# A transformer trunk on one core: the mixed stretch ordered by a planner in the kernel, plain products in a bank of the sevens

## The chip, the cores and the metric

The kernel runs on one core of a Trainium2 chip. The metric is the time of one execution on the device in microseconds (us), as the median of three runs. TensorE (PE) multiplies and loads its weights (PEld), VectorE (DVE), ScalarE (ACT) and GpSimd (POOL) do the elementwise work, and SyncE (SP) issues most of the transfers from the chip's memory.

## What is computed

Two layers of an encoder for 256 tokens of width 2048, in float32. Cut to what matters:

```python
for l in range(DEPTH):                      # 2
    h = rms_norm(x, ln1_g[l])
    o = two_attentions(h @ w_in[l])         # 8 + 8 heads of 128
    x = x + o @ w_out[l]
    h2 = rms_norm(x, ln2_g[l])
    u = depthwise_conv(h2 @ w_up[l], conv_w[l], conv_b[l])
    gate, up = u[..., :5632], u[..., 5632:]
    x = x + (silu(gate) * up) @ w_down[l]
```

The weights are most of the 412.80 MB that one execution reads.

## The kernel before

**Quanta and portions.** The weights come in quanta of 128 x 2048 numbers (1 MB), listed in `quanta` in the order in which TensorE uses them. A quantum is used in portions of 128 x 1024: two halves, or three *parts* for a seven. `steps` lists the portions. For each one TensorE needs a *high* part, the weight rounded to TensorE's fast 32-bit type, and a *low* part, the weight minus its high part. ScalarE makes the high part (tile `whi`, L114 or L807) and VectorE the low part (tile `wlo`, L115). For the second half of each plain and of the second quantum of each up, the low part comes another way (`by_transfer`): ScalarE writes the negated weight into `v_a` or `v_b` (L794), and GpSimd issues a DMA that adds the weight to it (L795), with the rounded sum as the low part. Activations are split in the same way, so a product of weights and activations takes three multiplications: high by high, low by high, high by low.

**The loop.** In step s, `low_w` prepares the low part by transfer of step s + 7 and `split_w` both parts of step s + 4 (five buffers each of `whi` and `wlo`). Three quanta are in SBUF at a time (`raw`); when the last portion of one is split, SyncE may load the next but two (L767), as soon as its tile is released.

**The feed-forward part.** A value of f, 0 to 43, stands for 128 columns of the gate and 128 of the other half. An *up* is two quanta: 32 matmuls of 512 and 32 of 256 columns into a tile `mm` of PSUM, the up's pair of banks. Then `glu` follows: ScalarE reads the pair into two tiles `prob` (L558, L559), VectorE adds them and scales them into `halo` (L560, L561), GpSimd copies the two halo edges (L563, L564), ScalarE and VectorE do the convolution (L569 to L573), then SiLU and gate, and the result is split into a *middle* tile. There are 26 middle tiles in five places (`MIDDLE`). For each pair of f, `sums_mid` makes four sums of the gated values (L589 to L592).

**Sevens and plains.** For the first 32 values of f, and in one half of the columns for 8 more, the product with `w_down` takes a form with seven products in place of eight, in chunks of eight f and for two halves m of the columns. One *seven* handles a pair of f in three parts of six matmuls, each 512 wide. VectorE makes the sums of its weights in place (L773 to L775, before part 1 is split). Four sevens add up in seven banks of PSUM: products 1 and 6 are the two banks of one tile `mm`, 5 and 7 take `S`, 3 takes `tr`, 4 takes `pv`. Then `add_seven` (L636 to L644) adds the banks to x: ScalarE copies product 1 (L637) into `tq`, VectorE reads the rest. The products with the fourth block of the weights are left to a *plain*, one quantum and 12 matmuls for each chunk and m, into a bank of its own in a tile `mm` (of which there are two, shared with the ups and sevens), and VectorE adds it to x (L673).

**The order.** In the list, nine ups come first. Then for each m the plain stands ahead of four pairs of a seven and an up:

```python
while f < PART + 1:
    quanta += up(f)
    f += 1
...
for m in range(2):
    quanta += plain(m)
    for i in range(PAIRS):
        quanta += seven(i, m) + up(f)
        f += 1
```

The last chunk (12 values of f) has one plain and four sevens, and its other products are `down` quanta. I call the time from the tenth up to the first `down` the *mixed stretch*; there is one in each layer. On each engine the instructions stand in an order that the scheduler of the language sets when the program is built, by its own estimate of durations and by the priorities in the code (`tc.high_priority`). The engines then run them in that order.

## Time and profile before

| what | value |
|---|---|
| median of three runs | 2200.76 us (2199.34 to 2203.48) |
| profiled execution | 2200.82 us |
| its span, first to last instruction | 2199.0 us |
| mean granted TensorE clock | 0.991 |
| PE busy | 2106.3 us, 96% |
| PEld busy | 1779.7 us, 81% |
| DVE busy | 1720.6 us, 78% |
| ACT busy | 1539.4 us, 70% |
| POOL busy | 221.8 us, 10% |

The profile is one execution, recorded instruction by instruction. A row of a group names a line, an engine, an operation, its output and inputs (the names of their tiles) and the shape, then how often it ran, how long together and on average. "A <- B: 24.6, 8, 3.5" in a view of waits says that A stood idle 24.6 us in all, in 8 places, 3.5 us at most, each time ended by B. PE's busy time counts overlapping matmuls as busy, so 96% does not mean that 4% is all that could be won. A view of windows gives the busy time of every engine in a stretch of the span.

### The profile page before, as it was taken

To read this page: it belongs to the slowest core of one execution; us is meant where nothing else is said; L and a number is where in the kernel's file an instruction comes from. 1 tells how busy PE (TensorE), PEld (TensorE's weight loads), DVE (VectorE), ACT (ScalarE), POOL (GpSimd) and SP (SyncE) were. 2 spreads that over 40 slices of the span, in tenths; PEclk is the share of its full clock that TensorE was granted. 3 is DMA by queue.
4 is the path that set the end of the run, shared out by engine and by line. 5 is a ranking of instruction groups with operands and counts; after the bars stand their busy time and mean duration, and the time that the engine had idled before them with its cause. 6 is when DMAs were issued, how large, how long until landed. Compare 5 with 4: busy or idle time off the path is not lost.

```text
span 2199.0 us, 29611 instructions
## 1 busy us (share of the span) xinstructions
PE 2106.3 (96%) x10720; PEld 1779.7 (81%) x10720; DVE 1720.6 (78%) x2522; ACT 1539.4 (70%) x2419; POOL 221.8 (10%) x343
## 2 busy tenths in 40 slices
PE   9999999999899998998999999999999999889999
PEld 7888888887778777777888888888877788777877
DVE  7786656778888888888857866667898889888886
ACT  7566558877777777777655665588777777777774
POOL 0011101110100001001000111011100001011000
PEclk9999999999999999999999999999999999999999
DMA  9555467776776677767655454577777777767774
GB/s 349 173 167 171 164 190 223 223 251 223 223 228 221 220 230 230 228 211 225 243 182 182 156 175 163 185 223 218 262 226 230 230 229 237 224 211 231 258 225 154
DMA packets 78563, 472.40 MB, mean 215 GB/s; under 512 B 9168, under 2 KB 11728, under 8 KB 29136
## 3 DMA queue, kind: packets, MB, share of 16 engines
q1 hardware_dynamic: 62432, 413.85, 52.1%
q0 software_dynamic: 15264, 55.58, 13.9%
q8 instruction: 84, 1.38, 0.2%
q10 hardware_dynamic: 720, 1.08, 0.1%
q14 instruction: 63, 0.52, 0.1%
HBM read 412.80 MB, written 2.10 MB: 189 GB/s over the span
## 4 chain that ended last, share of the span: by engine, by line
PE 48%; DMA 22%; DVE 19%; ACT 6%; issue 5%; ACTq 0%; SPq 0%; POOLq 0%; DVEq 0%
PE mm L100 42%; DVE wlo L115 9%; DMA raw<-in_w_up 9%; DMA raw<-in_w_seven 5%; DMA raw<-in_w_plain 4%; ACT whi L114 4%; DMA v_b<-raw 2%; DVE raw L773 2%; DMA v_a<-raw 2%; PE pv L100 2%; PE S L100 2%; DVE pT L573 1%; DVE raw L775 1%; PE tr L377 1%; DVE mid L115 1%
## 5 line engine op out<-in xcount | busy, mean ns | idle before, releaser
L115 DVE TENSOR_TENSOR wlo<-raw,whi 128x1024 fp32r<-128x1024 f32 (+1 forms) x739 | 893.1, 1221 | 336.0 <-ACT whi L114 307.9
L100 PE MATMUL mm<-xs,whi 128*128 128x512 f32 x2816 | 987.2, 393 | 8.4 <-ACT prob L559 8.1
L114 ACT ACTIVATE whi<-raw 128x1024 fp32r<-128x1024 f32 (+1 forms) x739 | 765.1, 1052 | 328.8 <-PE mm L100 182.2
L100 PEld LDWEIGHTS mm<-xs,whi 128*128 128x128 f32 x2816 | 530.5, 188 | 126.3 <-ACT prob L559 17.4
L100 PE MATMUL mm<-xs,wlo 128*128 128x256 f32 x2112 | 599.8, 284 | 2.7 <-DVE wlo L115 2.6
L100 PEld LDWEIGHTS mm<-xs,wlo 128*128 128x128 f32 x2112 | 401.8, 190 | 12.0 <-DVE wlo L115 10.0
L100 PE MATMUL mm<-whi,mid 128*128 128x512 f32 x1032 | 290.0, 404 | 48.6 <-DVE tq L638 30.0
L100 PE MATMUL mm<-whi,xs 128*128 128x512 f32 x1152 | 294.9, 393 | 1.3 <-ACT whi L114 1.2
L100 PEld LDWEIGHTS mm<-whi,mid 128*128 128x128 f32 x1032 | 195.8, 194 | 97.7 <-DVE tq L638 33.8
L100 PEld LDWEIGHTS mm<-whi,xs 128*128 128x128 f32 x1152 | 213.0, 188 | 43.7 <-ACT whi L114 2.2
L100 PE MATMUL mm<-wlo,xs 128*128 128x512 f32 x576 | 158.8, 393 | 0.0
L100 PE MATMUL mm<-wlo,mid 128*128 128x512 f32 x480 | 149.2, 399 | 3.8 <-DVE wlo L115 3.8
L571 ACT ACTIVATE pT<-halo,conv 128x256 f32<-128x256 f32 x352 | 149.4, 496 | 3.6 <-POOL halo L563 3.5
L573 DVE TENSOR_TENSOR pT<-pT 128x512 f32<-128x512 f32 x176 | 121.3, 689 | 30.2 <-ACT pT L571 25.9
L100 PEld LDWEIGHTS mm<-wlo,xs 128*128 128x128 f32 x576 | 107.2, 188 | 21.4
L807 ACT ACTIVATE whi<-raw 128x1024 fp32r<-128x1024 f32 x106 | 111.3, 1050 | 2.6 <-PE mm L100 2.0
L100 PEld LDWEIGHTS mm<-wlo,mid 128*128 128x128 f32 x480 | 91.4, 191 | 25.1 <-DVE wlo L115 6.2
L100 PE MATMUL mm<-xs,v_b 128*128 128x256 f32 x352 | 99.3, 282 | 0.0
L100 PE MATMUL mm<-xs,v_a 128*128 128x256 f32 x352 | 99.3, 282 | 0.0
L794 ACT ACTIVATE v_a<-raw 128x1024 fp32r<-128x1024 f32 x53 | 55.9, 1056 | 60.8 <-DMA raw<-in_w_up 42.6
L795 POOL DMA_DIRECT2D v_a<-raw x53 | 46.2, 871 | 508.0 <-ACT v_a L794 340.2
L795 POOL DMA_DIRECT2D v_b<-raw x53 | 46.1, 870 | 502.7 <-ACT v_b L794 343.0
(223 smaller groups left out, 2529.2 us busy)
## 6 DMA issues: line engine op xcount, KB each, us to landing
raw<-in_w_up SPq DMA_DIRECT2D x176, 1024.0 KB, 6.3
raw<-in_w_seven SPq DMA_DIRECT2D x72, 1024.0 KB, 5.7
raw<-in_w_in SPq DMA_DIRECT2D x71, 1024.0 KB, 4.9
raw<-in_w_out SPq DMA_DIRECT2D x32, 1024.0 KB, 4.9
v_a<-raw POOLq DMA_DIRECT2D x53, 512.0 KB, 4.8
v_b<-raw POOLq DMA_DIRECT2D x53, 512.0 KB, 4.9
raw<-in_w_plain SPq DMA_DIRECT2D x18, 1024.0 KB, 5.9
raw<-in_w_down SPq DMA_DIRECT2D x16, 1024.0 KB, 4.9
```

The source lines that it names most:

```text
L100: nc.tensor.matmul(ps, lhsT, rhs, start=start, stop=stop, skip_group_check=True)
L114: high = nc.scalar.activation(hi, src, AF.Copy)
L115: nc.vector.tensor_sub(lo, src, hi.bitcast(F32))
L377: nc.tensor.transpose(ps[:, kt, tt * P:(tt + 1) * P], p[:, tt, kt * P:(kt + 1) * P], ident)
L571: nc.scalar.activation(n[:, j, :], ux[:, j, o:o + T], AF.Copy, scale=w)
L573: nc.vector.tensor_add(y, y, n)
L773: nc.vector.tensor_sub(w[:, 1:3], w[:, 1:3], w[:, 2:4])
L775: nc.vector.tensor_sub(w[:, 0], w[:, 3], w[:, 0])
L794: nc.scalar.activation(lo, src, AF.Copy, scale=-1.0)
L795: nc.gpsimd.dma_start(out=lo, in_=src, accum_op=ALU.add)
L807: highs[s] = nc.scalar.activation(hl[s][0], raw[q][:, half * 1024:(half + 1) * 1024], AF.Copy)
```

## The change

A class `Plan` keeps a list of the instructions to come on each engine, with what they need, an estimated cost and a time at which they are due. It takes one at a time: of those that can begin within 0.1 us of the earliest on their engine, the one due first. Within the mixed stretch (from f = 1 of each layer to the first `down`) the order of PE, ACT, DVE and POOL is what it puts out (`tc.manual_schedule`); SP's stays the scheduler's. The other edits:

- The plain of a pair of chunk and m comes after its four sevens, and multiplies into the bank of product 1 (`cur["seven"][1]`), once ScalarE has copied that product (`copy_seven`, after part 0 of the last seven). Its own addition to x is gone. The nine additions of `add_seven` are each due at a time of their own.
- The halo edges are copied by ScalarE, in two instructions (`sides`).
- A quantum is loaded in two halves of 512 KB, into six tiles of half the size, and inside the mixed stretch a seventh in the place of `tabs`, a table of attention. `kT` holds a sixth high part. The sums of a seven's weights become four instructions of 512 columns in place of one of 1024 and two of 512, with results in `prob_a`, which GpSimd clears again for each layer.
- Three middle tiles fewer (23); three of a pair's four are given back early. Eight ups come first, not nine. `EARLY` is 6.

The numbers of instructions: TensorE's matmuls stay at 10632. VectorE's TensorTensor go from 2031 to 2085, ScalarE's ACTIVATE from 2317 to 2493, SyncE's transfers from 430 to 815, GpSimd's copies from 176 to 0.

The diff, cut to its core:

```diff
-MIDDLE = (("mid", MIDS), ("qT", 3), ("qtok", 3), ("kT", 2), ("kTb", 1))
+MIDDLE = (("mid", MIDS), ("qT", 3), ("qtok", 3))
-EARLY = 7
+EARLY = 6
...
+    def act(self, key, n, due, fn, deps=(), pointers=0, when=None):
+        self.op(key, "ACT", 0.12 + 0.00084 * n + 0.09 * pointers, due, fn, deps, when)
+
+    def dve(self, key, n, due, fn, deps=(), k=1, when=None):
+        self.op(key, "DVE", k * (0.075 + 0.00105 * n), due, fn, deps, when)
+
...
+    def run(self, stop):
+        while stop in self.ops:
+            best = {}
...
+            for eng, c in best.items():
+                first = min(c)[0] + 0.1
+                due, t, key = min((due, t, key) for t, due, key in c if t <= first)
+                if pick is None or t < pick[0]:
+                    pick = t, key
+            t, key = pick
+            eng, dur, _, fn, _, _ = self.ops.pop(key)
+            self.free[eng] = t + dur
+            self.now = self.done[key] = t + dur + self.LATE
+            fn()
...
-        nc.gpsimd.tensor_copy(ux[:, :, 1:r], ux[:, :, T:T + r - 1])
-        nc.gpsimd.tensor_copy(ux[:, :, T + r:T + 2 * r - 1], ux[:, :, r + 1:2 * r])
...
+        def scale():
+            nc.vector.tensor_mul(ux[:, :, r:r + T], own[0], st["r2"][:, None, :].to_broadcast([P, 2, T]))
+
+        def sides():
+            nc.scalar.activation(ux[:, :, 1:r], ux[:, :, T:T + r - 1], AF.Copy)
+            nc.scalar.activation(ux[:, :, T + r:T + 2 * r - 1], ux[:, :, r + 1:2 * r], AF.Copy)
...
+        plan.act(k("t"), 512, e + 2.5, lambda: read(0), [("pe", q, 1), k("gate", f - 1)])
+        plan.act(k("t2"), 512, e + 3.0, lambda: read(1), [k("t"), k("sum", f - 1)])
+        plan.dve(k("sum"), 512, e + 5.0, lambda: nc.vector.tensor_add(own[0], own[0], own[1]), [k("t"), k("t2")])
+        plan.dve(k("scale"), 512, e + 6.0, scale, [k("sum")] + [k(n + str(j), f - 2) for n in "yab" for j in range(2)])
+        plan.op(k("sides"), "ACT", 0.3, e + 7.0, sides, [k("scale")])
...
+                plan.act(k(n + str(j)), T, e + 7.5 + i % 3 + 0.5 * j, lambda n=n, j=j, o=o, i=i: tap(n, j, o, i),
+                         [k(dep), old], 2 if n == "y" else 1)
...
+        plan.dve(k("gate"), T, e + 14.0, gate, [k("silu")] + old)
+        plan.act(k("high"), T, e + 18.0, high, [k("gate")], when=lambda: sum(free.values()) > 0)
+            todo = (((1, gs[f][:, :, a], 1), (3, ss[p, 3], 0)),
+                    ((7, ss[p, 2], 0), (5, ss[p, 0], 1)),
+                    ((4, gs[f + 1][:, :, b], 0), (6, ss[p, 1], 1)))[part]
...
-                    drop(l, p)
+                    drop(l, p, (0, 2, 3))
                 if i == PAIRS - 1:
-                        add_seven(m, ps)
+                    add_seven(l, c, m, q, ps)
+            if part == 0 and i == PAIRS - 1:
+                copy_seven(l, c, m, q, ps)
...
+    def copy_seven(l, c, m, q, ps):
...
+            nc.scalar.activation(cur["t"], ps[1], AF.Copy)
+
+        plan.act(k("copy"), 512, ends.get(q, 0.0) - 2.2, copy, [("pe", q, 0), k("x2_", 1)])
...
+    def add_seven(l, c, m, q, ps):
...
+        last = [("pe", q + 1, 1)]
...
-        nc.vector.tensor_add(x11, x11, ps[1])
-        nc.scalar.activation(t, ps[1], AF.Copy)
-        nc.vector.tensor_add(t, t, ps[6])
-        nc.vector.tensor_add(x12, x12, t)
-        nc.vector.tensor_add(x12, x12, ps[3])
-        nc.vector.tensor_add(x_2, x_2, both(ps[5]))
-        nc.vector.tensor_add(t, t, ps[7])
-        nc.vector.tensor_add(x2_, x2_, both(t))
-        nc.vector.tensor_sub(x21, x21, ps[4])
+        add = nc.vector.tensor_add
+
+        plan.dve(k("x12b"), 512, e + 11.0, lambda: add(x12, x12, ps[3]), [("pe", q, 2)])
+        plan.dve(k("x_2"), 1024, e + 13.4, lambda: add(x_2, x_2, both(ps[5])), [("pe", q, 2), k("x12b")])
+        plan.dve(k("x11"), 512, e + 11.5, lambda: add(x11, x11, ps[1]), last)
+        plan.dve(k("t6"), 512, e + 12.0, lambda: add(cur["t"], cur["t"], ps[6]), last + [k("copy")])
+        plan.dve(k("x12"), 512, e + 13.6, lambda: add(x12, x12, cur["t"]), [k("t6"), k("x_2")])
+        plan.dve(k("t7"), 512, e + 14.0, lambda: add(cur["t"], cur["t"], ps[7]), [k("x12")])
+        plan.dve(k("x2_"), 1024, e + 22.0, lambda: add(x2_, x2_, both(cur["t"])), [k("t7"), k("x_2"), k("x21")])
+        plan.dve(k("x21"), 512, e + 15.0, lambda: nc.vector.tensor_sub(x21, x21, ps[4]), [("pe", q, 2)])
...
-            if half == 0:
-                cur["dn"] = psum.tile([P, TT, 512], F32, name="mm", bufs=2)
-            ps = cur["dn"][:, 0]
+            ps = cur["seven"][1]
...
-                       half == 0 and i == 0 and x_part == 0 and w is hv, half == 1 and i == 1 and w is lv)
-            if half == 1:
-                xv = x[:, 0, m * 1024:m * 1024 + 512]
-                nc.vector.tensor_add(xv, xv, ps)
...
-            while f < PART + 1:
...
+            while f < PART:
                 quanta += up(f)
                 f += 1
-            if nf == PART:
-                for m in range(2):
-                    quanta += plain(m)
-                    for i in range(PAIRS):
-                        quanta += seven(i, m) + up(f)
-                        f += 1
-            else:
-                quanta += plain()
+            for m in range(2 if nf == PART else 1):
                 for i in range(PAIRS):
-                    quanta += seven(i)
+                    quanta += seven(i, m)
+                    if i == PAIRS - 1:
+                        quanta += plain(m)
                     if f < NF:
                         quanta += up(f)
                         f += 1
...
-            raw[q] = wp.tile([P, 2048], F32, name="raw", bufs=3)
...
+    def load(parts=1, home="raw"):
+        if loaded[0] < len(halves):
+            q, h = k = halves[loaded[0]]
+            loaded[0] += 1
...
+                raw[k] = wp.tile([P, 1024], F32, name="raw", bufs=HALVES)
...
-        if part == 1:
-            nc.vector.tensor_sub(w[:, 1:3], w[:, 1:3], w[:, 2:4])
-            nc.vector.tensor_add(w[:, 3], w[:, 3], w[:, 1])
-            nc.vector.tensor_sub(w[:, 0], w[:, 3], w[:, 0])
-        return split(hv, lv, (w[:, 1::2], w[:, 1:3], w[:, 0::3])[part])
...
+    def free_raw(k):
+        del raw[k]
+        home = homes.pop(k)
+        if home == "raw" or plan.active:
+            load(1, home)
...
+    def sums_first(q):
+
+        zs[q] = act.tile([P, 3 * TT * T], F32, name="prob_a")[:, 0:1024]
+        z, u, w = pair(zs[q]), pair(raw[q, 0]), pair(raw[q, 1])
+        nc.vector.tensor_sub(z[:, 0], u[:, 0], w[:, 0])
+        nc.vector.tensor_sub(z[:, 1], w[:, 0], u[:, 1])
+
+    def sums_second(q):
...
+        nc.vector.tensor_add(u[:, 1], u[:, 1], z[:, 0])
+        nc.vector.tensor_sub(u[:, 0], u[:, 1], w[:, 1])
+        free_raw((q, 1))
...
+        plan.act(high, 1024, due - HI, lambda: high_w(s), need + prev + full, when=here)
+        plan.dve(low, 1024, due - LO, lambda: low_w_dve(s), [high] + order[-1:] + slot())
...
+        if kind == "seven" and part == 0:
+            plan.dve(("z", q), 512, due - Z1, lambda: sums_first(q), from_raw + [("raw", q, 1)] + zlast, 2, when=both)
+            zlast[:] = [("low_w", s + 1), ("z2", q)]
+            plan.dve(("z2", q), 512, due - Z2, lambda: sums_second(q), [("z", q), high, low], 2)
...
+        if kind == "plain":
+            l, c, m = a
+            return w + [("copy", l, 2 * c + m)] + list(needs_plain(l, c, part))
+        return w
...
+            region.enter_context(tc.manual_schedule(engines={
+                mybir.EngineType.PE, mybir.EngineType.Activation, mybir.EngineType.DVE, mybir.EngineType.Pool}))
+            start_plan(s)
...
+        if plan.active:
+            if ("pe", q, half) in plan.ops:
+                plan.run(("pe", q, half))
+        else:
+            low_w(s + EARLY)
+            split_w(s + SPLIT_AHEAD - 1)
+            split_w(s + SPLIT_AHEAD)
```

**In the program.** The rows below stand at one place on three engines: layer 0, the end of the first four sevens (m = 0 of the first chunk). Names end in the number of the tile.

TensorE before: the last two matmuls of an up (xs are its activations), then the plain, whose tile mm_4797 is its own.

```order
L100 MATMUL mm_4686<-xs15_3109,whi_4662 128x512
L100 MATMUL mm_4686<-xs15_3109,v_b_4578 128x256
L100 MATMUL mm_4797<-whi_4682,mid_3320 128x512
L100 MATMUL mm_4797<-whi_4682,mid_3553 128x512
L100 MATMUL mm_4797<-whi_4682,mid_3320 128x512
L100 MATMUL mm_4797<-whi_4682,mid_3553 128x512
L100 MATMUL mm_4797<-wlo_4683,mid_3320 128x512
L100 MATMUL mm_4797<-wlo_4683,mid_3553 128x512
L100 MATMUL mm_4797<-whi_4703,mid_3786 128x512
L100 MATMUL mm_4797<-whi_4703,mid_4022 128x512
```

TensorE after: the third part of the last seven (products 4 in pv and 6 in mm), then the plain; mm_4152 is the tile of products 1 and 6, and kT_4596 is a high part in the added place.

```order
L165 MATMUL pv_4156<-whi_4593,mid_4283 128x512 x2
L165 MATMUL pv_4156<-wlo_4598,mid_4283 128x512
L165 MATMUL mm_4152<-whi_4593,mid_4350 128x512 x2
L165 MATMUL mm_4152<-wlo_4598,mid_4350 128x512
L165 MATMUL mm_4152<-kT_4596,mid_3530 128x512
L165 MATMUL mm_4152<-kT_4596,mid_3771 128x512
L165 MATMUL mm_4152<-kT_4596,mid_3530 128x512
L165 MATMUL mm_4152<-kT_4596,mid_3771 128x512
L165 MATMUL mm_4152<-wlo_4627,mid_3530 128x512
L165 MATMUL mm_4152<-wlo_4627,mid_3771 128x512
```

Before, this is the plain of m = 1, ahead of its sevens; after, that of m = 0, right behind its sevens and ahead of the up, in the sevens' tile.

VectorE before: the first pass over product 6 (L638, after ScalarE's copy into tq_4672) among the sums of the next seven's weights (L773 to L775), the sums of the middle (L589 to L592) and low parts (L115).

```order
L773 TENSOR_TENSOR raw_4641<-raw_4641 128x1024
L589 TENSOR_TENSOR tq_4626<-bias_4475,bias_4621 128x128
L115 TENSOR_TENSOR kT_4623<-bias_4621,kT_4623 128x256
L638 TENSOR_TENSOR tq_4672<-tq_4672,mm_4178 128x512
L774 TENSOR_TENSOR raw_4641<-raw_4641 128x512
L590 TENSOR_TENSOR tq_4626<-tq_4626,bias_4475 128x128
L115 TENSOR_TENSOR wlo_4744<-raw_4641,whi_4743 128x1024
L639 TENSOR_TENSOR x_70<-x_70,tq_4672 128x512
L775 TENSOR_TENSOR raw_4641<-raw_4641 128x512
L592 TENSOR_TENSOR tq_4626<-bias_4621,tq_4626 128x128
L560 TENSOR_TENSOR prob_4766<-prob_4766,prob_4767 128x512
L115 TENSOR_TENSOR qT_4631<-tq_4626,qT_4631 128x256
```

VectorE after: the additions to x (L799 to L803), low parts (L1006), the convolution (L687), the gate (L666) and the sums of weights (L958, L959).

```order
L799 TENSOR_TENSOR x_70<-x_70,tr_4155 128x512
L1006 TENSOR_TENSOR wlo_4720<-tabs_4501,whi_4683 128x1024
L687 TENSOR_TENSOR pT_4697<-pT_4697,pT_4700 128x512
L687 TENSOR_TENSOR pT_4697<-pT_4697,pT_4725 128x512
L801 TENSOR_TENSOR x_70<-x_70,mm_4152 128x512
L666 TENSOR_TENSOR bias_4754<-prob_4643,pT_4697 128x256
L802 TENSOR_TENSOR kTb_4653<-kTb_4653,mm_4152 128x512
L1006 TENSOR_TENSOR wlo_4759<-raw_4600,kT_4752 128x1024
L800 TENSOR_TENSOR x_70<-x_70,S_4153 128x2x512
L958 TENSOR_TENSOR raw_4600<-raw_4600,prob_a_4671 128x512
L959 TENSOR_TENSOR raw_4600<-raw_4600,raw_4620 128x512
L803 TENSOR_TENSOR x_70<-x_70,kTb_4653 128x512
```

The additions to x now alternate with the work of the up and with low parts.

ScalarE before: high parts (L114, L807) and the convolution (L569, L571), then the copy of product 1 (L637) and the first read of the up's pair (L558).

```order
L569 ACTIVATE pT_4609<-halo1_112,conv_468 128x256 x2
L571 ACTIVATE pT_4610<-halo1_112,conv_468 128x256 x2
L571 ACTIVATE pT_4611<-halo1_112,conv_468 128x256 x2
L114 ACTIVATE whi_4723<-raw_4641 128x1024
L574 ACTIVATE prob_4601<-pT_4609 128x256
L114 ACTIVATE kT_4623<-bias_4621 128x256
L637 ACTIVATE tq_4672<-mm_4178 128x512
L114 ACTIVATE whi_4743<-raw_4641 128x1024
L558 ACTIVATE prob_4766<-mm_4686 128x512
```

ScalarE after: the two reads of the up's pair (L646), the copy of product 1 (L784, into kTb_4653), a negation (L982), high parts (L997), the halo edges (L652, L653) and the convolution.

```order
L646 ACTIVATE prob_4643<-mm_4513 128x512
L997 ACTIVATE whi_4645<-raw_4475 128x1024
L784 ACTIVATE kTb_4653<-mm_4152 128x512
L646 ACTIVATE prob_4659<-mm_4513 128x512
L982 ACTIVATE v_a_4667<-raw_4541 128x1024
L997 ACTIVATE whi_4674<-raw_4497 128x1024
L997 ACTIVATE whi_4683<-tabs_4501 128x1024
L652 ACTIVATE halo0_115<-halo0_115 128x2x3
L653 ACTIVATE halo0_115<-halo0_115 128x2x3
L660 ACTIVATE pT_4697<-halo0_115,conv_483 128x256
L662 ACTIVATE pT_4700<-halo0_115,conv_483 128x256 x2
```

The copy has moved between the two reads of the up, and the halo edges stand ahead of the convolution that reads them.

More of the change, by code (lines that the diff above doesn't have):

```diff
@@ new lines, in free_raw @@
+    def free_raw(k):
[3 more added lines that the diff above has]
+            load(1, home)
+            if plan.active and loaded[0] < len(halves):
+                k2 = halves[loaded[0] - 1]
+                plan.issued = max(plan.issued, plan.now, plan.done.get(("sent", *k), 0.0))
+                plan.dma(("raw", *k2), plan.issued, 1.55, 2.0)
+    kind_of = lambda s: quanta[steps[s][0]][2]
+    is_seven = lambda s, part: s < len(steps) and kind_of(s) == "seven" and steps[s][1] == part
@@ L781, in by_transfer, with source @@
+    def source(s):
+        q, part = steps[s]
+        if kind_of(s) == "seven":
+            return zs[q] if part == 1 else raw[q, 0]
+        return raw[q, part]
     def by_transfer(s):
@@ L821, in encoder_kernel @@
+                    free_raw(steps[s])
+                else:
+                    high_w(s)
+                    low_w_dve(s)
     xT = []
```

375 lines of the change are left out of this document (283 added, 92 removed).

## The prediction

> **What bounds the kernel now.** I begin with the busy time by stretch, because the page's mean hides that the stages have different limits. The columns are the stretch, its length, then busy time (and instructions) of TensorE, its weight loads, VectorE, ScalarE and GpSimd, the granted TensorE clock, the share of the DMA engines and GB/s.
>
> ```profile
> 0.00:323.00 323.00, 320.49 (x1555) 269.04 (x1556) 229.92 (x443) 196.64 (x343) 34.60 (x36) 1.00 0.59 201
> 338.80:419.28 80.48, 80.48 (x467) 71.43 (x466) 55.56 (x83) 69.27 (x114) 13.38 (x21) 1.00 0.78 233
> 419.28:1015.70 596.42, 549.70 (x2813) 460.92 (x2812) 500.43 (x676) 444.55 (x670) 61.81 (x110) 0.98 0.71 224
> 1520.80:2104.90 584.10, 544.97 (x2814) 459.64 (x2812) 500.23 (x676) 444.51 (x670) 59.92 (x110) 0.99 0.72 229
> 580.00:630.00 50.00, 48.73 (x258) 41.63 (x259) 45.18 (x59) 38.62 (x58) 3.81 (x9) 1.00 0.71 231
> 2030.00:2080.00 50.00, 49.78 (x263) 42.28 (x262) 45.09 (x58) 40.10 (x61) 4.45 (x9) 1.00 0.74 234
> ```
>
> Attention and the first ups keep TensorE busy throughout: nothing can be won there. The two mixed stretches, where sevens, plains and ups alternate, do not. Matmuls overlap, so busy time flatters them; how long their matmuls need without a wait comes from two dense stretches. The first rows are the same view for the matmuls of the ups alone (operand xs), the last is a piece of the chain that ended last, in order of time.
>
> ```profile
> 338.80:419.28 80.48, 80.48 (x466) 1.00 0.78 233
> 419.28:1015.70 596.42, 377.08 (x2114) 0.98 0.71 224
> 1520.80:2104.90 584.10, 379.51 (x2115) 0.99 0.72 229
> 10.35 65.62 PE mm L100 x288
> ```
>
> An up's matmul takes 80.48 / 466 = 0.1727 us, a 512-wide one of the other kind 65.62 / 288 = 0.2278 us. The first mixed stretch has 2114 of the one and 2813 - 2114 = 699 of the other: 365.1 + 159.3 = 524.4 us, against 596.4. The second, with 2115 and 699, needs 524.6 against 584.1. So 72.0 + 59.5 = **131.5 us of slack** is all this change can touch. Who is waited for, by TensorE's weight loads, in the first and then the second stretch (total, times, longest):
>
> ```profile
> PEld mm L100 <- DVE tq L638: 24.6, 8, 3.5
> PEld mm L100 <- ACT whi L114: 12.5, 8, 2.8
> PEld mm L100 <- ACT prob L559: 12.3, 14, 2.0
> PEld mm L100 <- DVE wlo L115: 10.1, 12, 1.5
> PEld S L100 <- DVE x L641: 6.3, 7, 0.9
> PEld mm L100 <- DVE tq L638: 19.3, 8, 3.3
> PEld mm L100 <- ACT whi L114: 17.9, 7, 3.1
> PEld mm L100 <- DVE wlo L115: 7.6, 12, 1.1
> PEld S L100 <- DVE x L641: 6.2, 8, 0.9
> PEld mm L100 <- ACT prob L559: 4.9, 9, 1.1
> ```
>
> These are 65.8 + 55.9 = 121.7 us; the other 9.8 is the granted clock of 0.98 and 0.99. Two kinds stand here. A free bank is awaited in tq L638 (43.9 together), x L641 (12.5) and prob L559 (17.2): short reads of PSUM that come late in their engine's order. Weight portions are awaited in whi and wlo (48.1): the supply. Behind that supply stand other waits, of ScalarE for transfers, of VectorE for ScalarE and of SyncE's queue for VectorE (from 422 to 1015 us):
>
> ```profile
> ACT whi L114 <- DMA raw<-in_w_seven: 30.7, 16, 3.7
> ACT v_a L794 <- DMA raw<-in_w_up: 24.9, 12, 3.3
> ACT v_b L794 <- DMA raw<-in_w_up: 14.5, 11, 2.9
> ACT v_a L794 <- DMA raw<-in_w_plain: 9.6, 4, 2.6
> ACT v_b L794 <- DMA raw<-in_w_plain: 9.0, 4, 2.3
> DVE wlo L115 <- ACT whi L114: 78.5, 48, 3.7
> SPq L767 <- DVE wlo L115: 417.3, 88, 12.0
> ```
>
> SyncE, which issues the loads, stands idle 417.3 us until VectorE has freed a raw tile. So the loop is: tile freed late, load late, high part late, low part late, TensorE late. No engine is full; the loop is out of step.
>
> **The change, part by part.** *TensorE*: as many matmuls as before, 12 per plain. The term is 0; only the waits move.
>
> *The plains' bank.* The plain no longer asks for a tile of its own, and with that the tq wait before it goes: 43.9 us. In its place it waits for the ScalarE copy of the first product. Between that product's last matmul and the plain's first lie 12 matmuls, 12 x 0.2278 = 2.7 us, and the copy takes 578 ns. If ScalarE is up to 2.1 us behind, the wait is hidden. If it is not, TensorE stands, and on ScalarE the second PSUM read of the up, a negation and the next high parts are queued behind the copy. Bounds: 0, and 18 copies at the longest wait seen, 3.5 us, 63 us. I take 0, since the copy now stands ahead of those, and keep the cost for the range. The next seven needs both PSUM reads of the pair, but has a whole up (64 x 0.1727 = 11.1 us) for them.
>
> *VectorE.* The plain's add to x goes; the sums of a seven become four instructions of 512 in place of one of 1024 and two of 512. Rows by instruction, from 422 to 1015 us (L365 and L832 from the whole run):
>
> ```profile
> L773 DVE TENSOR_TENSOR raw<-raw 128x1024 f32<-128x1024 f32 x33 | 40.3, 1222 | 0.6
> L774 DVE TENSOR_TENSOR raw<-raw 128x512 f32<-128x512 f32 x33 | 22.6, 686 | 0.0
> L673 DVE TENSOR_TENSOR x<-x,mm 128x512 f32<-128x512 f32 x9 | 6.1, 682 | 0.0
> L637 ACT ACTIVATE tq<-mm 128x512 f32<-128x512 f32 x8 | 4.6, 578 | 0.0
> L365 ACT ACTIVATE es<-nm,sink 128x2 f32<-128x2 f32 x16 | 4.5, 281 | 0.0
> L832 ACT ACTIVATE junk<-halfpi 128x1 f32<-128x1 f32 x1 | 0.2, 203 | 0.0
> L563 POOL COPY halo<-halo 128x6 f32<-128x6 f32 x34 | 20.8, 613 | 156.3 <-DVE halo L561 156.3
> ```
>
> Per stretch that is 33 x (4 x 0.686 - 1.222 - 2 x 0.686) = +5.0 and -6.1, so 500.4 becomes 499.3 us. Against TensorE's 524.4 this is **95.2%**: with TensorE dense, VectorE has 25 us to idle, where it now has 96. This is the term that decides.
>
> *ScalarE* takes the halo edges, two instructions for each of 34 values of f. No row shows a 128x6 one; the nearest are 203 and 281 ns, so 13.8 to 19.1 us, and I take 14: 444.6 + 14 = 459, 87.5% of 524.4, hidden in its idle time. GpSimd loses copies that waited 156.3 us for VectorE, though scarcely anything waited for them; what gains is the accumulating transfers queued behind them.
>
> *Loads* come in halves: six tiles of 512 KB in the place of three of 1 MB, and a seventh (tabs). Bytes are the same, issues double (212 x 0.33 us = 70 us on SyncE, which idles 417). What matters is the round: 52 halves per 8 ups and 8 sevens, whose 512 + 168 matmuls are 126.7 us dense, so one per 2.4 us, and seven tiles give each 17.1 us for landing, splitting and release. Three whole tiles, one per 4.9 us, gave 14.6, and held a seven's whole megabyte to its third part. Landing times:
>
> ```profile
> raw<-in_w_up SPq DMA_DIRECT2D x65, 1024.0 KB, 6.5
> v_a<-raw POOLq DMA_DIRECT2D x21, 512.0 KB, 4.8
> bias<-in_bias SPq DMA_DIRECT2D x16, 160.0 KB, 3.4
> ```
>
> A half should land between 3.4 and 6.5 us; I take 4.8, the row of its size. That leaves 12.3 us for use, against 8.1 now. At the slow end 10.6 are left, still more.
>
> Here a page speaks against the change. The Trainium skill's "DMA: Bandwidth & Descriptors", section "Measured (HBM→SBUF, 128 partitions, SWDGE, issued from GpSimd)", says to batch transfers to at least 1 MiB, and times 1 MB at 6.15 us and 64 KB at 0.95. The 6.5 us above agree. Interpolated, an estimate, two halves would take 6.8 us, 10% more: a DMA share of 0.71 would become 0.89 of a dense stretch (0.71 x 596.4 x 1.1 / 524.4), not full. So the sum stays, but by that rule the fourth rival below is a real one.
>
> *Small moves at no cost.* Middle tiles drop from 26 to 23; 16 of a chunk and 8 of the next are wanted just before the first seven of the second half gives three back. What then waits is needed a chunk's half later, four times a seven and an up (18 x 0.2278 + 64 x 0.1727 = 15.2 us), and that hides it; without it, ScalarE would hold up high parts. Clearing prob_a once a layer falls on GpSimd in attention, where it is busy 34.6 of 323 us.
>
> *The order.* ScalarE and VectorE now follow due times, and the planner counts with durations near the rows' (0.98 us for a 1024-wide copy, where rows give 1.05 apart). The late PSUM reads have due times of 2.5 to 15 us, ahead of work due at 24 to 33, so I expect most of the 73.6 us of bank waits to go, while portions remain the limit, with VectorE's fullness as the measure. Rows bound it: its fullest 50 us reach 45.18 / 50 = 90.4%, and TensorE's own pace would demand 95.2%. I take **92%**, nearer to what a row shows. Then the stretches take 499.3 / 0.92 = 542.7 and 499.1 / 0.92 = 542.5 us, saving 53.7 + 41.6 = **95.3 us**. The span goes from 2199.0 to 2103.7. Around it the profiled execution had 1.8 us (2200.82 in all; the median of three is 2200.76, the same), so **2105.5 us**. The rest that TensorE waits is 36 us, mostly at the first portions of a seven.
>
> **The rivals.**
>
> 1. *Only the bank counts.* Portions wait as before, and only tq and x go: 43.9 + 12.5 = 56.4 us, 2144 us. For it: VectorE idles mostly for ScalarE, and ScalarE for transfers, which no order makes faster. Against it: the 417.3 us in which loads wait for a tile. The longest waits, 3.3 to 3.5 us, are the tq ones. The Trainium skill, "TensorE: Matmul & The Clock Gate", section "Part 1: The HAM clock gate", has the clock halved after an idle window of about 3.4 us; the clock of 0.98 agrees, and by that rule this rival would regain 9.8 us more, 2135.
> 2. *TensorE bound.* All slack goes: 2200.8 - 131.5 = 2069 us. It asks VectorE for 95.2% over 525 us, which no 50 us show.
> 3. *Nothing changes.* The waits only move: the copy costs what the tile did, and portions are late at other steps. 2200 us. TensorE's waits have five causes, none above 25 of 66 us, which speaks for this a little.
> 4. *Slower: halves that land late.* In the fixed ScalarE order every high part and negation holds back all behind it until its raw has landed. ScalarE waited 30.7 + 24.9 + 14.5 + 9.6 + 9.0 = 88.7 us over the 106 quanta loaded in the first stretch (65 ups, 33 sevens, 8 plains), 0.84 us each. If each half waits that long, it is 212 x 0.84 = 178 us; with 459 busy ScalarE needs 637 us, 41 over today's first stretch and 53 over the second: 2295 us. It decides from (596.4 - 459) / 212 = 0.65 us per half. Against it: a half is freed and asked for earlier, and 160 KB land in 3.4 us, so the wait should shrink with the size.
>
> **How the numbers follow.** Forecast (VectorE at 90.4 to 94%, 2083 to 2125 us): 0.62. Rival 1 (2125 to 2165): 0.15; rival 2 (2069 to 2080): 0.08; rival 3 (2165 to 2205): 0.05; rival 4: 0.10. The range runs from 2072 to 2165: it holds forecast, rival 1 and most of rival 2, and takes in part of the copy's 63 us; the third and fourth stay out. A measurement can tell about 0.2%, 4.4 us, from no change. Faster: 0.62 + 0.15 + 0.08 = 0.85; rival 3 is the same, 0.05; rival 4 slower, 0.10.
>
> **What would show it.** The wait for tq is gone, and no wait of over 1 us for the copy stands in its place. VectorE's busy share in the mixed stretches is 90 to 94%, its busy time within 3 us of 499. The clock is 0.99 or 1.00. SyncE's idle time before loads grows relative to ScalarE's waits for raw, which fall below 60 us a stretch; a half lands in 3.5 to 5.5 us. Ups and attention stay as long as they are. I am wrong if ScalarE waits over 130 us a stretch for raw (rival 4), if VectorE stays under 88% though the tq wait is gone (rival 1), or if the copy is awaited at most of the 18 plains.

## The result, and the profile after

The changed kernel takes **2090.47 us** (median of four runs, 2087.48 to 2091.0) where the one before takes 2200.41: a ratio of 0.9495, with a 95% interval of 0.9479 to 0.9512. The profiled execution took 2090.57 us and its span 2088.5, so 110.5 us of span are gone. The forecast was 2105.5.

First the view of windows, with the columns of before: attention, the dense ups, the mixed stretch of each layer, and the end. The stretches now run from the end of the eighth up, at 419.28 and 1459.70 us, to the read of the last up.

```profile
0.00:323.00 323.00, 321.50 (x1555) 269.94 (x1556) 227.67 (x427) 197.57 (x343) 33.66 (x36) 1.00 0.64 204
338.80:419.28 80.48, 80.48 (x466) 71.33 (x465) 59.42 (x90) 68.96 (x128) 6.12 (x7) 1.00 0.82 235
419.28:1002.50 583.22, 578.21 (x3068) 495.13 (x3067) 540.76 (x755) 483.92 (x790) 39.62 (x47) 1.00 0.84 249
1459.70:2041.70 582.00, 576.66 (x3066) 495.16 (x3065) 540.05 (x755) 484.07 (x790) 38.15 (x44) 1.00 0.84 251
```

Attention and the dense ups stand as they did. A mixed stretch holds 36 ups, 36 sevens and nine plains: 36 x 64 = 2304 matmuls at the 0.1727 us of the prediction and 36 x 18 + 9 x 12 = 756 at 0.2278 need 397.9 + 172.2 = 570.1 us without a wait. The stretches take 583.2 and 582.0, so **25 us of slack are left in the two together**. VectorE is busy 540.76 of 583.22 us, **92.7%**, and the clock is 1.00.

Who is waited for, by TensorE's weight loads, in the whole run (total, times, longest):

```profile
PEld mm L165 <- ACT prob L646: 19.3, 25, 1.3
PEld pv L165 <- DVE wlo L1006: 3.4, 7, 0.8
PEld S L165 <- DVE wlo L1006: 1.1, 3, 0.6
PEld mm L165 <- DVE wlo L1006: 0.4, 1, 0.4
```

The waits for tq and x are gone, and the copy of product 1 (L784) stands in no row. Behind TensorE, in the first mixed stretch, from 422 to 1002 us (the rows that bear on the loads and on VectorE):

```profile
ACT v_b L982 <- DMA raw<-in_w_up: 12.5, 8, 2.4
ACT v_a L982 <- DMA raw<-in_w_up: 11.7, 9, 2.7
DVE wlo L1006 <- ACT whi L997: 13.2, 14, 1.9
DVE prob_a L952 <- DMA raw<-in_w_seven: 11.7, 10, 2.5
DVE bias L666 <- ACT prob L689: 8.7, 9, 1.4
SPq L930 <- DVE wlo L1006: 126.8, 85, 5.7
SPq L930 <- DVE raw L959: 93.9, 23, 5.5
SPq L930 <- DVE bias L666: 76.3, 16, 6.3
SPq L930 <- DVE mid L673: 74.7, 23, 4.0
```

ScalarE's waits for raw were 88.7 us and are some 30; VectorE, which now reads a seven's halves first, waits 11.7 us for them. VectorE's waits for high parts were 78.5 us and are 13.2. SyncE waits about as long for VectorE as it did (417.3 us before, 371.7 in these rows), but in pieces of at most 6.3 us where 12.0 was the longest. The DMA queue of the loads before and after (packets, MB, share of 16 engines' span), and landings after:

```profile
q1 hardware_dynamic: 62432, 413.85, 52.1%
q1 hardware_dynamic: 117872, 413.87, 60.6%
raw<-in_w_up SPq DMA_DIRECT2D x302, 512.0 KB, 5.2
v_a<-raw POOLq DMA_DIRECT2D x46, 512.0 KB, 6.4
```

### The profile page after: what moved, and what is told of

Its sections match the earlier page's. It is cut to its first block, busy times and chain, and to the rows that moved or that the text cites. A ratio compares the mean times of both kernels' runs of the same rounds, so it can differ in the third digit from the quotient of the medians.

```text
span 2088.5 us, 30567 instructions
## 1 busy us (share of the span) xinstructions
PE 2072.3 (99%) x10720; PEld 1767.6 (85%) x10720; DVE 1711.1 (82%) x2576; ACT 1548.8 (74%) x2595; POOL 157.3 (8%) x170
## 3 DMA queue, kind: packets, MB, share of 16 engines
q1 hardware_dynamic: 117872, 413.87, 60.6%
## 4 chain that ended last, share of the span: by engine, by line
PE 62%; DVE 18%; DMA 11%; issue 5%; ACT 4%; DVEq 0%; ACTq 0%; POOLq 0%; SPq 0%
PE mm L165 55%; DVE wlo L1006 8%; DMA raw<-in_w_up 5%; DMA raw<-in_w_seven 3%; PE S L165 2%; ACT whi L997 2%; PE pv L165 2%; DVE pT L687 1%; PE tr L165 1%; DMA tabs<-in_w_up 1%; DVE halo L649 1%; DVE prob L677 1%; DVE raw L958 1%; DVE x L800 1%; DVE x L805 1%
## 5 line engine op out<-in xcount | busy, mean ns | idle before, releaser
L165 PE MATMUL mm<-xs,whi 128*128 128x512 f32 x2320 | 813.2, 391 | 9.3 <-ACT prob L646 9.1
L1006 DVE TENSOR_TENSOR wlo<-raw,whi 128x1024 fp32r<-128x1024 f32 x535 | 651.5, 1220 | 187.1 <-ACT whi L997 161.9
L997 ACT ACTIVATE whi<-raw 128x1024 fp32r<-128x1024 f32 x613 | 640.1, 1054 | 212.6 <-PE mm L165 169.3
L165 PEld LDWEIGHTS mm<-xs,whi 128*128 128x128 f32 x2320 | 435.2, 188 | 109.7 <-ACT prob L646 19.3
L165 PE MATMUL mm<-whi,mid 128*128 128x512 f32 x928 | 255.4, 393 | 0.4 <-ACT v_a L330 0.4
L165 PEld LDWEIGHTS mm<-whi,mid 128*128 128x128 f32 x928 | 169.9, 188 | 34.1 <-ACT v_a L330 0.9
L165 PE MATMUL mm<-xs,kT 128*128 128x512 f32 x496 | 174.6, 390 | 0.0
L662 ACT ACTIVATE pT<-halo,conv 128x256 f32<-128x256 f32 x352 | 157.7, 496 | 0.0
L687 DVE TENSOR_TENSOR pT<-pT 128x512 f32<-128x512 f32 x176 | 121.0, 687 | 12.3 <-ACT pT L660 4.1
L646 ACT ACTIVATE prob<-mm 128x512 f32<-128x512 f32 x176 | 102.4, 584 | 30.5 <-PE mm L165 29.5
L165 PEld LDWEIGHTS mm<-xs,kT 128*128 128x128 f32 x496 | 93.1, 188 | 19.5
L660 ACT ACTIVATE pT<-halo,conv 128x256 f32<-128x256 f32 x176 | 103.4, 589 | 0.0
```

The source lines that it names most:

```text
L165: nc.tensor.matmul(ps, lhsT, rhs, start=start, stop=stop, skip_group_check=True)
L646: nc.scalar.activation(own[part], ps[:, :, part], AF.Copy)
L660: nc.scalar.activation(own["y"][:, j], src, AF.Identity, scale=taps[j][i], bias=taps[j][3])
L662: nc.scalar.activation(own[name][:, j], src, AF.Copy, scale=taps[j][i])
L687: lambda n=n: nc.vector.tensor_add(own["y"], own["y"], own[n]),
L997: highs[s] = nc.scalar.activation(his[s], source(s), AF.Copy)
```

## The experiments

The theory to be tested is the prediction's: the order and the supply of portions together bring the gain, up to the point where VectorE is about 92% full. Its rivals are that the bank does it alone, that some other edit does, and that another engine is the limit now.

### One part at a time

The edits are cut to their core.

**e1**, on the kernel before:

```diff
+                with tc.high_priority(offset=4 * AHEAD_PRIO):
+                    nc.scalar.activation(cur["t"], ps[1], AF.Copy)
...
-            ps = cur["dn"][:, 0]
+            ps = cur["seven"][1]
...
-                    quanta += plain(m)
                     for i in range(PAIRS):
-                        quanta += seven(i, m) + up(f)
+                        quanta += seven(i, m)
+                        if i == PAIRS - 1:
+                            quanta += plain(m)
+                        quanta += up(f)
```

> The kernel before, with one edit: the plain comes after its four sevens and adds up in the bank of product 1, which ScalarE copies after part 0 of the last seven; the plain's own addition to x is gone. Loads, halo edges and the scheduler's order as before. If the bank is what counts (rival 1), the waits for tq (24.6 + 19.3 us) and x L641 (6.3 + 6.2 us) go and nothing takes their place: 2144 us. If the order and the supply of portions count, the waits move to the portions behind them: 2165 to 2200 us, and the wait for tq is gone all the same.

Measured: 2232.63 us, a ratio of 1.0132 (1.0105 to 1.0159): 1.3% slower, clear of the noise, where neither theory had a loss. TensorE's waits in this kernel, by its weight loads over the whole run:

```profile
PEld mm L100 <- DVE wlo L115: 48.4, 47, 1.5
PEld mm L100 <- ACT whi L114: 42.0, 50, 1.6
PEld mm L100 <- DMA v_a<-raw: 16.6, 8, 3.1
PEld mm L100 <- DMA v_b<-raw: 15.2, 7, 3.0
```

The wait for tq is gone, as expected, and so is that for x. In these rows 122 us are waits for portions, where the kernel before had 32.6 + 18.3 us in its two of this kind. So in this program the waits have moved to the supply. The scheduler set the whole order anew for it, so it is shown what TensorE waits for, but not whether the bank or the new order costs the 32 us.

**e2**, the changed kernel without the planner. The seventh tile and the sixth high part, which exist only inside the planned stretch, go with it, and there is one middle tile more:

```diff
-    first = {q - 2 * (PART - 1) for q in first}
+    first = set()
```

> The changed kernel without its planner: every edit stays (bank, half loads, sums in four instructions, halo edges on ScalarE), but the order is the scheduler's from the code's order and priorities. Outside the planner there is no seventh tile for halves and no sixth high part, and the free place of the latter serves as a 24th middle tile. If the planner's order is what brought most of the 110 us, this stays above 2150 us, with waits for tq or prob and for whi and wlo of over 40 us a stretch. If the other edits are enough, it comes below 2115 us.

Measured: 2191.17 us, 0.9953 (0.9937 to 0.9968). These edits without the planner bring a tenth of the gain. The first mixed stretch in the view of windows, then the waits of the weight loads, whole run:

```profile
419.30:1049.90 630.60, 590.05 (x3065) 493.33 (x3064) 543.17 (x758) 480.66 (x792) 39.60 (x47) 1.00 0.80 234
PEld mm L165 <- ACT prob L649: 46.5, 39, 2.0
PEld mm L165 <- ACT kTb L787: 32.3, 17, 2.7
PEld mm L165 <- DVE wlo L1012: 24.8, 28, 2.0
```

VectorE has the work of the changed kernel (543.17 us against 540.76), but is 86.1% full. TensorE waits 78.8 us for the up's reads and the copy, and 45.6 for portions (two rows of 12.2 and 8.1 and one of 0.5 us beside these). The copy of product 1 (kTb) is awaited before 17 of 18 plains, 1.9 us each: the cost that the prediction bounded at 63 us and put at nothing exists, and the planner's order is what hides it.

**e3**, the changed kernel with the plain in its own bank; the additions of products 1 and 6 are due 1.5 and 1.0 us after the last seven, since the next up waits for them:

```diff
-            ps = cur["seven"][1]
+            if half == 0:
+                cur["dn"] = psum.tile([P, TT, 512], F32, name="mm", bufs=2)
+            ps = cur["dn"][:, 0]
...
+                plan.dve(("xp", l, 2 * c + m), 512, ends.get(q, 0.0) + 8.0, lambda: nc.vector.tensor_add(xv, xv, ps), [("pe", q, 1)])
```

> The changed kernel with the plain back in a tile of its own, ordered by the planner: VectorE adds it to x (9 instructions of 0.68 us a layer), products 1 and 6 are added at once, and the next up waits for these two in the place of the plain's bank. If the order does away with bank waits by itself, the additions hide in VectorE's idle time (42 us a stretch): 2090 to 2103 us. If the bank is needed for it, the 43.9 us of before return: about 2134 us.

Measured: 2103.78 us, 0.9557 (0.9536 to 0.9578). The old wait of 43.9 us does not return. For the addition that now frees the bank, TensorE waits, whole run:

```profile
PEld mm L165 <- DVE x L801: 3.5, 3, 1.6
```

The kernel is 13 us slower than the changed one, about the 12.3 us that 18 additions more take VectorE. That they are the reason fits what e5 shows below, but is not shown apart from the other due times.

**e4**, without the seventh tile, and **e9**, in addition with halves asked for only in pairs:

```diff
-        load(1, "tabs")
```

```diff
-        if home == "raw" or plan.active:
+        gone.append(k)
+        if len(gone) % 2:
+            return
+        for _ in range(2):
             load(1, home)
```

> The changed kernel without the seventh tile (tabs), so with six halves in SBUF, as many bytes as the three whole quanta of before. Per half 6 x 2.4 = 14.6 us for landing, splitting and release in place of 17.1; a half lands in 5.2 us, so 9.4 us are left for use. If the order counts and the supply has room: 2090 to 2100 us. If the supply is the tight term: ScalarE's waits for raw double at least (27 us in the first stretch now) and the time is 2115 us or more.

> The changed kernel, in which the two halves of a quantum are asked for together, once both tiles of an earlier quantum are free: three quanta in SBUF and the round of before, no seventh tile, the planner's order for all else. If releasing halves one by one is what loosens the supply, this loses that (8.1 us for use per quantum in place of 9.4 per half without the seventh tile): 2130 us or more, with ScalarE waiting over 60 us a stretch for raw. If the order alone counts, it stays with the run without the seventh tile: 2105 to 2115 us.

Measured: e4 2109.77 us, 0.9582 (0.9562 to 0.9602); e9 2115.00 us, 0.9616 (0.9583 to 0.9649). The seventh tile is worth 19 us; e4 lies between its two theories (up to 2100, from 2115). e2 and e4 both have six tiles, and differ by the planner, with the sixth high part and one middle tile: 81 us. e9 is 5 us slower than e4, but the intervals overlap, so what the release of halves one by one adds is not settled. With the round of before (e9), 85 of the 110 us are still there. In both TensorE begins to wait for the accumulating transfers; the waits of its weight loads in e9, whole run:

```profile
PEld mm L165 <- DMA v_a<-raw: 18.3, 16, 2.2
PEld mm L165 <- DMA v_b<-raw: 17.8, 14, 2.5
```

These are 36 us, nearly all its waits. Not run were the planner on the kernel before with no other edit, and the planner with loads of 1 MB.

**e8**, halo edges back on GpSimd:

```diff
-            nc.scalar.activation(ux[:, :, 1:r], ux[:, :, T:T + r - 1], AF.Copy)
+            nc.gpsimd.tensor_copy(ux[:, :, 1:r], ux[:, :, T:T + r - 1])
...
-        plan.op(k("sides"), "ACT", 0.3, e + 7.0, sides, [k("scale")])
+        plan.op(k("sides"), "POOL", 1.3, e + 7.0, sides, [k("scale")])
```

> The changed kernel with the halo edges back on GpSimd, in the planner's order (1.3 us for both in its reckoning). If they were hidden on either engine, as the prediction took it, nothing moves: 2086 to 2096 us. If they get in the way of the DMAs that GpSimd issues for the low parts, TensorE waits for v_a and v_b: 2100 us or more.

Measured: 2087.23 us, 0.9480 (0.9460 to 0.9501): no change. The edges are hidden on either engine.

**e10**, the kernel before with each load as two DMAs:

```diff
-    def load(q, parts=1):
+    def load(q, parts=2):
```

> The kernel before, in which each quantum's load is issued as two DMAs of 512 KB into the two halves of its one tile; all else as it was. If halves cost the DMAs 10% (the page's rule, interpolated), the share of 0.71 grows to 0.78 in the mixed stretches and the time to 2205 us or more. If a first half that lands earlier (5.2 us in the changed kernel) is what counts, ScalarE's waits for raw shrink and it is 2170 to 2192 us. If the waits for a free tile hide both, 2196 to 2205 us.

Measured: 2252.92 us, 1.0234 (1.0205 to 1.0262). Slower by 53 us, on the side of the first theory. The queue of the loads is busy 54.0% of 2252.2 us, 1216 us, where it was 52.1% of 2199.0, 1146: 6% more. ScalarE's waits for raw over the whole run grow from 70.1 + 42.6 + 37.3 us to the first three rows below; the last two are TensorE's waits that grew most, from 43.9 and 17.9 us:

```profile
ACT whi L114 <- DMA raw<-in_w_seven: 89.6, 46, 3.8
ACT v_a L794 <- DMA raw<-in_w_up: 63.7, 34, 4.1
ACT v_b L794 <- DMA raw<-in_w_up: 59.9, 31, 3.7
PEld mm L100 <- DVE tq L638: 58.4, 16, 4.4
PEld mm L100 <- ACT prob L559: 46.0, 43, 2.6
```

So TensorE's added waits are for late reads of banks, not for portions. The scheduler's order is another one here too, so how much of the 53 us is the halves and how much the order stays open.

### What is the limit now

**e5** and **e6**: VectorE's scaling twice for each f (the edges and the convolution wait for the second), and one sum fewer for each seven, so that e6 leaves out a part of the computation.

```diff
+        plan.dve(k("again"), 512, e + 6.0, again, [k("scale")])
```

```diff
-        nc.vector.tensor_sub(u[:, 0], u[:, 1], w[:, 1])
```

> The changed kernel with VectorE's scaling into halo done twice for each f (88 more instructions of 0.685 us, 24.7 us in each mixed stretch of 36 ups, which the planner knows of). The result is the same. If VectorE's fullness is the measure, as the prediction took it (540.8 of 583.2 us, 92.7%), the stretches grow to 565.5 / 0.927 = 610 us: about 2144 us. If TensorE is the limit now and VectorE has its 42 us to spare, less than a third of that comes back: 2091 to 2108 us, with the low parts awaited more than the 5 us of now.

> The changed kernel without the last of the four sums of each seven's weights (72 instructions of 0.686 us fewer, 24.7 us a stretch); part 2 uses the weights without it, so the output is not the reference's. If VectorE's fullness is the measure, the stretches could fall to TensorE's own pace, 570 us: about 2066 us. If TensorE is the limit and its last waits are the reads of the up's banks by ScalarE (19.3 us of 26), only the waits for low parts go, 4.9 us: 2083 to 2091 us.

Measured: e5 2158.3 us, 0.9796 (0.9764 to 0.9829), beyond the 2144 of its first theory; e6 2074.38 us, 0.9419 (0.9393 to 0.9444), between its two. The first mixed stretch of e5, with TensorE's longest wait in the whole run, then that of e6:

```profile
427.20:1033.90 606.70, 584.75 (x3054) 494.65 (x3055) 561.91 (x789) 480.47 (x789) 39.62 (x47) 0.99 0.82 239
PEld mm L165 <- DVE wlo L1010: 43.6, 39, 3.5
```

```profile
419.20:997.00 577.80, 575.47 (x3065) 495.75 (x3064) 519.17 (x720) 481.82 (x790) 39.72 (x47) 1.00 0.84 252
```

With 21 us more of work VectorE is 92.6% full, as in the changed kernel, and the stretch is 23.5 us longer. In the second one 22 us more make it 28.8 us longer, at 92.0% (562.20 of 610.80 us from 1497.70). So what VectorE gets to do comes back one to one or a little more, and TensorE waits for its low parts. With 22 us less the stretch shortens by 5.4 us only, to 7.7 us above TensorE's own 570.1. So **the changed kernel stands on the knee**: VectorE at its 92 to 93% and TensorE 2% above its pace, both at once. The rest of e5's loss lies in the dense ups, which take 8 us longer in each layer. Of the 42 us in which VectorE is idle in the changed kernel's first stretch, 33.6 are the three waits shown above, for ScalarE and for loads: it is not full because what it works on comes late.

**e7**, the up's reads due earlier:

```diff
-        plan.act(k("t"), 512, e + 2.5, lambda: read(0), [("pe", q, 1), k("gate", f - 1)])
-        plan.act(k("t2"), 512, e + 3.0, lambda: read(1), [k("t"), k("sum", f - 1)])
+        plan.act(k("t"), 512, e + 0.5, lambda: read(0), [("pe", q, 1), k("gate", f - 1)])
+        plan.act(k("t2"), 512, e + 0.6, lambda: read(1), [k("t"), k("sum", f - 1)])
```

> The changed kernel with the two reads of an up's banks due 0.5 and 0.6 us after its end in place of 2.5 and 3.0. If the remaining slack is late reads (prob L646, 19.3 us), it goes for the most part: 2071 to 2081 us. If ScalarE has no place for them there, high parts come late in their stead and the time stays: 2086 to 2097 us.

Measured: 2089.24 us, 0.9492 (0.9471 to 0.9512): no change. The wait for prob falls from 19.3 us, and one for the copy stands beside it:

```profile
PEld mm L165 <- ACT prob L646: 13.6, 25, 1.1
PEld mm L165 <- ACT kTb L784: 3.0, 10, 0.6
```

Taking 5.7 us out of the longest row of waits brought nothing that can be measured.

**e11** and **e12** were to give VectorE less to do with the computation whole: the sums of gated values on GpSimd (one of the four is shown), and more low parts by transfer.

```diff
-            nc.vector.tensor_add(v[:, 0], m1[:, b], m2[:, b])
+            nc.gpsimd.tensor_add(v[:, 0], m1[:, b], m2[:, b])
```

```diff
+        if half == 1 and quanta[q][2] == "up" and quanta[q][3][1] >= PART and quanta[q][3][1] % 2 == 0:
+            return True
```

> The changed kernel with the four sums of gated values of each pair (128x128, 0.284 us each, 20 us of VectorE a stretch) on GpSimd, in the planner's order (3.2 us for the four in its reckoning). The result is the same. If VectorE's fullness is the measure, as the runs with more and with less work for it have it (24.7 us a stretch less gave 16 us), the time falls to 2075 to 2081 us. If the sums take longer on GpSimd than their middles can wait, or hold up the DMAs that it issues, or slow VectorE down, it is 2088 us or more.

> The changed kernel, in which the second half of the first quantum of every other up from f = 8 gets its low part by transfer as well: 36 more negations on ScalarE (1.06 us) and accumulating DMAs, 36 fewer subtractions on VectorE (1.22 us, 22 us a stretch). The result is the same. If VectorE's fullness is the measure, this gives nearly what the run with one sum fewer gave (16 us for 24.7 us a stretch): 2074 to 2081 us. If what VectorE loses is needed at ScalarE (484 + 19 of 583 us) or the transfers (6.4 us to land) come late, TensorE waits for v_a and v_b or for high parts: 2088 us or more.

Measured: e11 2105.97 us, 0.9564 (0.9541 to 0.9587); e12 2136.59 us, 0.9709 (0.9681 to 0.9737). Both slower than the changed kernel. By line, the low parts of the first mixed stretch in the changed kernel and in e11, and the first of the sums in e11 over the whole run (min/median/max in ns):

```profile
L1006 DVE TENSOR_TENSOR wlo<-raw,whi x134: 1210/1218/1228, 420.9 to 1000.7; 128x1024 fp32r<-128x1024 f32 x134
L1006 DVE TENSOR_TENSOR wlo<-raw,whi x130: 1212/1222/1489, 421.1 to 998.9; 128x1024 fp32r<-128x1024 f32 x130
L710 POOL TENSOR_TENSOR tq<-bias x40: 454/1253/1432, 365.9 to 2003.3; 128x128 f32<-128x128 f32 x40
```

So VectorE and the sums on GpSimd hold each other up: a sum of 454 ns takes 1253 at the median, a low part up to 261 ns longer, and the subtraction behind a middle tile (L673, 74 times) 678 ns at the median in place of 418. While VectorE stood idle (530.73 to 532.08 us), sums took 0.45 and 0.46 us. In the changed kernel the 160 sums took VectorE 45.8 us; without them its busy time fell by 7.0 us only (1711.1 to 1704.1). TensorE then waits 24.2 us for low parts (13.6 + 7.9 + 2.7), where it waited 4.9.

In e12 VectorE has 36 subtractions fewer, and the loads wait for the transfers instead (whole run):

```profile
SPq L930 <- DMA v_a<-raw: 319.4, 62, 11.0
SPq L930 <- DMA v_b<-raw: 319.3, 62, 10.6
PEld mm L165 <- DMA v_b<-raw: 24.2, 10, 4.0
PEld mm L165 <- DMA v_a<-raw: 19.2, 10, 4.4
```

In the changed kernel SyncE waited 79.4 and 81.0 us for the first two. A half that goes by transfer holds its raw tile until the transfer has landed (7.6 us here at the median, 6.4 in the changed kernel), and tiles are scarce, as e4 shows. The DMA engines are also fuller, 0.88 of the first stretch in place of 0.84; how much of the 46 us is the tiles and how much this stays open. No run that computes the whole result beats the changed kernel by more than the measurement tells: the best, e8, is 3 us below it with overlapping intervals.

## Why the prediction was right, and where not

- *Slack as the size of what can be won*: right. 131.5 us were named and 110.5 taken. The named windows ended three ups ahead of the end of a layer. From the read of the ninth up to that of the last, the timelines of before (start, length) have

```profile
430.56 0.58 ACT L558 ACTIVATE prob<-mm 128x512 f32<-128x512 f32 x1
...
1060.79 0.57 ACT L558 ACTIVATE prob<-mm 128x512 f32<-128x512 f32 x1
...
1532.02 0.58 ACT L558 ACTIVATE prob<-mm 128x512 f32<-128x512 f32 x1
...
2149.92 0.58 ACT L558 ACTIVATE prob<-mm 128x512 f32<-128x512 f32 x1
```

  which is 630.2 and 617.9 us for 35 ups, 35 sevens and nine plains, 555.0 us without a wait: 138.2 us of slack, 7 more than named.
- *No wait for tq, no copy awaited*: right, both. But the shared bank, to which the prediction gave the 43.9 us, is not what did it. With a bank of its own the plain costs 13 us under the planner (e3), and the shared bank in the scheduler's order went with a loss of 32 us (e1). That the copy costs nothing was given a reason, its place in ScalarE's order; e2, where it is awaited 32.3 us, shows that the place is needed.
- *The order and the supply of portions decide*: shown. e2 leaves 10 of 110 us; with the same six tiles the planner and its sixth high part bring 81 more (e4), and the seventh tile 19.
- *VectorE's fullness as the measure, at 92%*: right for the changed kernel. It came out at 92.7% and held at 92.6 and 92.0% when VectorE got more work (e5). Its work in terms of TensorE's pace came out as worked out: 540.76 / 570.1 = 94.9%, against 95.2%. The 92% itself was picked between two bounds, and no row gave it, so that it came this near is in part luck. The lower bound was misread: 45.18 us are not the fullest 50 us of before, since from 1737 to 1787 us VectorE was busy 45.95, 91.9%. And the share is no constant of the kernel: with six tiles and halves in pairs it is 91.5% (e9, 547.46 of 598.40 us), with more transfers 87.3% (e12, 527.43 of 604.20), and there TensorE waits for transfers.
- *The size*: 15 us too small. VectorE at 92% would make the stretch 540.76 / 0.92 = 587.8 us, and 583.2 were measured: 4.6 us a stretch, 9 in both. The 7 us that the windows missed make about the rest.
- *What TensorE still waits for*: wrong. It was to be the first portions of a seven; it is the read of an up's banks, 19.3 of some 25 us. An earlier due time takes only 5.7 us from it (e7).
- *Halves land in 3.4 to 6.5 us, at 4.8*: 5.2 for an up's. The queue of the loads was busy 60.6% of 2088.5 us, 1266 us, against 1146: 10.5% more. The time fell all the same, since the DMA engines were not full (0.84). The Trainium skill's "DMA: Bandwidth & Descriptors", section "Measured (HBM→SBUF, 128 partitions, SWDGE, issued from GpSimd)", gave the estimate of 10% more DMA time for halves, by interpolation. The changed kernel agrees with it, e10 with its 6% less so; the table there is for DMAs issued from GpSimd, and these loads are issued from SyncE.
- *Seven tiles leave more time for use than three whole ones*: right, and tighter than thought: a tile fewer was still to leave 9.4 us for use against 8.1 before, yet costs 19 us (e4).
- *Halo edges at 14 us, hidden*: right (208 and 192 ns at the median, x 34, are 13.6 us; e8). That the transfers behind GpSimd's copies would gain by it was not borne out: with the copies back on GpSimd the time is the same (e8).
- *The rivals*: "only the bank" fell in e1 and e3. "TensorE bound" holds in part: 13 and 12 us above TensorE's pace are left in the stretches, and with less work for VectorE 7.7 in the first (e6). "Nothing changes, the waits only move" is near to what e1 shows, at a loss. "Halves that land late" fell for the changed kernel; in the scheduler's order (e10) ScalarE's waits for raw grew by 63 us and the time by 53, with the cause open as said there.

## What to carry to other kernels

Where several engines feed TensorE and none is full (in the first mixed stretch before, VectorE 84%, ScalarE 75%, the DMA engines 71%), edits that take single waits away may bring nothing (e7) or a loss (e1); an order by due times over all engines made nearly the same edits worth some nine times as much (e2 against e4). How full the busiest feeder can get gave the nearer forecast here, 15 us off where the sum of the slack would have been 21 us off; one case does not make that a rule. Once it stood at 92 to 93%, each us of work given to it came back one to one or more, and work moved off it gained nothing where the new place held it up (e11) or kept buffers that the loads needed (e12).

## What had not been expected of the hardware

- A GpSimd addition of 128x128 took 454 ns at best and 1253 ns at the median beside a VectorE busy 91% of the time, whose 128x1024 subtraction took up to 1489 ns beside it in place of at most 1228 (e11). The Trainium skill's "SBUF — State Buffer", section "SBUF: two separate sides", has a GpSimd instruction and a VectorE one with two SBUF inputs exclude each other; these numbers agree in kind, though a low part lost at most 261 ns at a time, less than a whole addition.
- Loads in halves made the DMA engines busy 10.5% longer in the changed kernel and 6% longer in the old one (e10), for the same bytes.
